# A fifth gate pair in the seven-product form, and GpSimd's share of the attention's elementwise work

## The chip, the cores and the metric

The kernel runs on one core of a Trainium2 chip. The metric is the device time of one execution in microseconds; less is better. The engines named below are PE (TensorE, the matmuls) with PEld (its weight loads), DVE (VectorE), ACT (ScalarE), POOL (GpSimd) and SP, whose queue issues nearly all DMAs.

## The reference

One decoder block on x of 1024 tokens by 1024 features, all float32:

```python
h = rms_norm(x, ln1_g)
proj = h @ w_in + b_in            # 1024 x 6400
rq, rk, rv, rg, aq, ak, av, gate_a, gate_b = jnp.split(proj, SPLIT_IDX, axis=-1)
ry = head_group_norm(retention_chunkwise(rotary(rq), rotary(rk), rv), ret_norm_g)
branch_a = (silu(rg) * ry) @ w_ret_out
ay = sliding_window_sink_attention(rotary(aq), rotary(ak), av, attn_sinks)
branch_b = ay @ w_attn_out
merged = sigmoid(gate_a) * branch_a + sigmoid(gate_b) * branch_b
x = x + merged @ w_out
h2 = rms_norm(x, ln2_g)
x = x + (silu(h2 @ w_ffn_gate) * (h2 @ w_ffn_up)) @ w_ffn_down
return rms_norm(x, lnf_g)
```

The attention has 16 query heads of 64 on 2 key/value heads, blocks of 128 queries against 256 keys (the block's own and the one before), a window of 128 and a learned sink for each head. The two gates have 1024 columns each, that is 16 groups of 128.

## The kernel before

**Products.** A float32 operand is kept as a high half (rounded to the matmul's fp32r) and a low half (the difference). A product is three matmuls: high by high, high by low, low by high. Weights are split after their load: `split` (L129) lets ACT write the high half (L130) and DVE the low (L133). `dense_g` (L176) does this for one group of 128 columns: load (L146), split, then for each half of the tokens 24 matmuls of 512 columns (`mm_g`, L157 to L159) and an evacuation. It is a generator: each `yield`, every three matmuls, is a step that other work can be put between.

**Stages.** By the trace: norm and the attention's k and v to 44 us; q of the first quad of heads to about 88; the attention to about 333, and what is left of its filling to 359; the retention's v from 359 to 435, and then, to 624, pairs of 128 columns (retention q and k, the swish gate, and some of the gates), both in a form with seven products of halves of the operands where eight would be usual (L841 for the pairs, their columns in `cols`, L599); the retention itself, the output projections and the FFN. Ten pairs run in the second of the seven-product stages: eight for the retention, two for gates 2 to 5.

**The attention.** 32 units, 4 quads of heads by 8 blocks; unit (g,b) is block b of quad g, and its tiles bear these digits (pv13 belongs to unit (1,3), sc16 to (1,6)). A unit goes through

- `u_scores`: four score products (PE L459, L460), the copy of the sink into each row (POOL L451), the masked row reduction (DVE L463), four exponentials with row sums (ACT L466), the reciprocal (DVE L469), and four scalings: columns 0 and 2 on DVE (L474), 1 and 3 on ACT (L472);
- `u_transpose`: eight transposes on PE (L484), the split by ACT (L487) and DVE (L488);
- `u_values`: the value products (PE L497, L498), copies and sums by ACT (L501, L502) and DVE (L503, L504), and a split back into q's place (L506, L507).

The loop runs unit i−1's transposes, unit i's scores, some steps of filling, and unit i−1's values. The **filling** (`Fill`, L187) is a list of generators: the q of the next quad (`quad_q`, L384: its weights L395 to L402, then 96 matmuls, the bias L409, the rotation on DVE L419 to L424, a split L425 to L428, a store L430 and a reload L432 through memory) and the gates (`gate`, L509: 48 matmuls, tanh L513, a store L514). Before a new quad begins, `until` runs the filling up to that quad's q. The weights of the filling are emitted under a raised priority (`AHEAD`); the order of each engine's instructions follows from these priorities, and each engine runs its own in order, as SP does its DMAs.

Two buffers (`wr`) hold raw weights, three PSUM banks (`acc`) the filling's results.

Of the kernel before, what the change touches and what calls it, by code (L numbers as in the profile page):

```python
# [14 lines left out]
ALU = mybir.AluOpType  # L15

P = 128
D = 1024
S = 1024
NB = S // P  # L20
# [10 lines left out]
C_RQ, C_RK, C_RV, C_RG, C_AQ, C_AK, C_AV, C_GA, C_GB = (  # L31
    0, 512, 1024, 2048, 3072, 4096, 4224, 4352, 5376)


def f32(t):
    return t.bitcast(F32)
# [3 lines left out]
def hybrid_block(ctx: ExitStack, tc: tile.TileContext, x, ln1_g, w_in, b_in, ret_norm_g, w_ret_out,  # L40
                 attn_sinks, w_attn_out, w_out, ln2_g, w_gate, w_up, w_down, lnf_g,
                 c_ident, c_atab, c_rtab, c_amask, c_rmask, c_rcol, out):
    nc = tc.nc
    x = x[0]
    out = out[0]
    w_in, w_ret_out, w_attn_out, w_out = w_in[0], w_ret_out[0], w_attn_out[0], w_out[0]
# [79 lines left out]

    held = []

    def split(raw, hi, lo, hold=False):  # L129
        nc.scalar.copy(hi, raw)  # L130

        def low():
            return nc.vector.tensor_tensor(out=lo, in0=raw, in1=f32(hi), op=ALU.subtract)  # L133
        if hold:
            held.append(low)
        else:
            return low()
# [2 lines left out]
        while held:  # L140
            held.pop(0)()

    def slab(src, col, name):
        with tc.high_priority(offset=AHEAD):
            raw = raw_slab([8, P], name)
            nc.sync.dma_start(raw, src[:, col:col + P].rearrange("(k p) n -> p k n", p=P))  # L146
            hi, lo = hl_tiles([8, P], name)
            split(raw, hi, lo)
        return hi, lo

    def mm_g(pt, w, X, c0, n=512):
# [21 lines left out]
        for i, (wt, k, u) in enumerate(todo):  # L173
            nc.tensor.matmul(pt, wt[:, k, :], X[k // 4][:, 2 * (k % 4) + u, c0:c0 + n], start=(i == 0), stop=(i == 23))

    def dense_g(src, col, X, evac, name):  # L176
        w = slab(src, col, name)
        for half in range(2):
            pt = acc(f"acc_{name}_{half}")
            yield from mm_g(pt, w, X, half * 512)  # L180
            evac(half, pt)
            yield
# [64 lines left out]
    for t in range(NB):  # L247
        if t > 1:
            nc.sync.dma_start(xs[:, t, :], x[t * P:(t + 1) * P, :])
        if 1 <= t <= 2:  # L250
            raw = raw_slab([8, P], f"kv{t}")
# [3 lines left out]
    H = [big(A, "A", 0, "h0"), big(A, "A", 1, "h1")]  # L255
# [45 lines left out]
    with tc.tile_pool(name="gt", bufs=1, side="right") as gt, tc.tile_pool(name="w1", bufs=1) as w1:  # L301
# [83 lines left out]
        def quad_q(g):  # L385
            if g % 2 == 0:
                big(B, "B", g // 2, f"q{g}")
            Bt = B[g // 2]
            jb = (g % 2) * 4
            w = [hl_tiles([8, P], f"aq{g}{z}") for z in range(2)]  # L390
            hp = tc.high_priority(offset=AHEAD)
            hp.__enter__()
            for kk in range(2):
                raw = raw_slab([4, 256], f"aq{g}{kk}")
                nc.sync.dma_start(raw, w_in[kk * 512:kk * 512 + 512, C_AQ + g * 256:C_AQ + g * 256 + 256]  # L395
                                  .rearrange("(k p) n -> p k n", p=P))
                rv_ = raw.rearrange("p k (j z e) -> p k z j e", j=4, z=2, e=32)
                for z in range(2):
                    hi = w[z][0][:, kk * 4:kk * 4 + 4, :].rearrange("p k (j e) -> p k j e", e=32)
                    lo = w[z][1][:, kk * 4:kk * 4 + 4, :].rearrange("p k (j e) -> p k j e", e=32)  # L400
                    nc.scalar.copy(hi, rv_[:, :, z])
                    nc.vector.tensor_tensor(out=lo, in0=rv_[:, :, z], in1=f32(hi), op=ALU.subtract)  # L402
            hp.__exit__(None, None, None)
            ab = {}
            for z, half in ((0, 0), (0, 1), (1, 0), (1, 1)):
                pt = acc(f"aq{g}{z}{half}")
                yield from mm_g(pt, w[z], H, half * 512)
                t = r512("ra" if z == 0 else "rb", 2 - z, f"q{g}{z}{half}")
                nc.scalar.activation(t, pt, AF.Identity, bias=bcol[:, QB + 4 * z + g:QB + 4 * z + g + 1], scale=1.0)  # L409
                ab[z, half] = t  # L410
                if z == 0:
                    yield
                    continue
                c = slice(half * 512, half * 512 + 512)
                a, b = ab[0, half], t
                stg = w1.tile([P, 4, 512], F32, tag="stg", bufs=1, name=f"stg{g}{half}")
                s0, s1, s2, s3 = (stg[:, i, :] for i in range(4))
                cos, sin = atab[:, 0, c], atab[:, 1, c]
                nc.vector.tensor_tensor(out=s2, in0=a, in1=cos, op=ALU.mult)  # L419
                nc.vector.tensor_tensor(out=s1, in0=b, in1=sin, op=ALU.mult)  # L420
                nc.vector.tensor_tensor(out=s2, in0=s2, in1=s1, op=ALU.subtract)
                nc.vector.tensor_tensor(out=s0, in0=a, in1=sin, op=ALU.mult)
                nc.vector.tensor_tensor(out=s3, in0=b, in1=cos, op=ALU.mult)
                nc.vector.tensor_tensor(out=s3, in0=s3, in1=s0, op=ALU.add)  # L424
                nc.scalar.activation(s0.bitcast(F32R), s2, AF.Copy)  # L425
                nc.vector.tensor_tensor(out=s2.bitcast(F32R), in0=s2, in1=s0, op=ALU.subtract)
                nc.scalar.activation(s1.bitcast(F32R), s3, AF.Copy)
                nc.vector.tensor_tensor(out=s3.bitcast(F32R), in0=s3, in1=s1, op=ALU.subtract)  # L428
                qd = q_d[2 * g + half]
                nc.sync.dma_start(qd, stg)  # L430
                for r in range(4):
                    nc.sync.dma_start(f32(Bt[r * 32:r * 32 + 32, jb:jb + 4, c]),  # L432
                                      qd[:, r, :].rearrange("(j e) c -> e j c", e=32))
                yield
# [9 lines left out]
        def u_scores(u):  # L444
# [23 lines left out]
            rd = tiny.tile([P, 4], F32, tag="rd", name=f"rd{g}{b}")  # L468
            nc.vector.reciprocal(rd, den)  # L469
            for j in range(4):  # L470
                if j % 2:
                    nc.scalar.activation(sc[:, j, 0:nk], sc[:, j, 0:nk], AF.Copy, scale=rd[:, j:j + 1])  # L472
                else:
                    nc.vector.tensor_scalar(out=sc[:, j, 0:nk], in0=sc[:, j, 0:nk], scalar1=rd[:, j:j + 1],  # L474
                                            scalar2=None, op0=ALU.mult)

        def u_transpose(u):
            g, b, nk, Bt, jb, qc = geo(u)
# [30 lines left out]
        def gate(n):  # L509

            def evac(half, pt):
                t = gt.tile([P, 512], F32, tag="st", bufs=2, name=f"tb{n}{half}")
                nc.scalar.activation(t, pt, AF.Tanh, bias=bhalf[:, n:n + 1], scale=0.5)  # L513
                nc.sync.dma_start(tb_d[n, :, half * 512:half * 512 + 512], t)  # L514
            return dense_g(w_in, C_GA + n * P, H, evac, f"g{n}")

        run(quad_q(0))
        order = list(range(6, 16))
        gens = []
        for g in range(4):  # L520
            gens += [quad_q(g + 1)] if g < 3 else []
            gens += [gate(n) for n in (order[2 * g:2 * g + 2] if g < 3 else order[6:] + [0, 1])]
        fl = Fill(gens)
        NU = 4 * NB
        fl.step(20)
        left = 32 * 8 - 8 - 20
        for i in range(NU + 1):
            if i % NB == 0 and 0 < i < NU:
                fl.until(3 * (i // NB - 1) + 1)
            if i > 0:  # L530
                u_transpose(i - 1)
            if i < NU:
# [63 lines left out]
        return [kq.tile([P] + shape, F32, tag=t, name=f"{name}{t}") for t in ("kT", "qT")]  # L596

    cols = [c for h in range(RH) for c in ((C_RK, C_RQ, C_RK + 256, C_RQ + 256)[h], C_RG + 256 * h)]
    cols += [C_GA + 256, C_GA + 512]  # L599
    NW = len(cols)  # L600

    with tc.tile_pool(name="rvp", bufs=1) as rvp:
# [706 lines left out]
    X = {}  # L1309
# [384 lines left out]
```

## Time and profile before

| | us |
|---|---|
| three runs | 1582.56, 1584.97, 1584.98 |
| median | 1584.97 |
| span of the profiled execution | 1583.3 |

No other time than its span is given for the profiled execution. In the windows, a row gives a stretch in us from the span's start, its length, and the busy time of each engine with its number of instructions. A busy time counts overlaps of neighbouring instructions once. A row of the groups gives line, engine, operation, tiles (out<-in), shapes, count, then total us and mean ns of one, then the idle time ahead of them and what ended it. A row of the waits gives who waited, for whom, the total, how often, and the longest.

### The profile page before, as it was taken

What the parts mean: (1) busy time and instruction counts of PE and PEld (TensorE: products, weight loads), DVE (VectorE), ACT (ScalarE), POOL (GpSimd) and SP (SyncE); (2) the same over time, 40 slices, a digit from 0 to 9 for tenths busy, and PEclk for the clock granted to TensorE, in tenths of its full rate; (3) what the DMA queues carried; (4) which work ended last, traced back from release to release, by engine and by line L of the source; (5) the groups of instructions that cost most, each with busy time, mean ns of one, the idle gap of its engine ahead of it and who ended that gap; (6) DMA issues with size and microseconds to landing.
All of it is one profiled execution on the core that took longest, in us unless ns stands there. A gap on an engine that the chain in (4) does not pass through costs nothing.

```text
span 1583.3 us, 20873 instructions
## 1 busy us (share of the span) xinstructions
PE 1570.7 (99%) x7483; PEld 1307.1 (83%) x7483; DVE 990.2 (63%) x1776; ACT 720.7 (46%) x1446; POOL 354.9 (22%) x303
## 2 busy tenths in 40 slices
PE   9999999999999999999999999999999999999998
PEld 8887888888888888888888888888888888888886
DVE  6469978777657663878544369444444444678656
ACT  5258877844233333544221256333333333344445
POOL 2000000000055441000000013555555555100001
PEclk9999999999999999999999999999999999999999
DMA  6564655440364455654545102333333333762333
GB/s 204 157 176 124 205 193 150 143 140 34 126 225 150 134 166 184 229 189 156 177 149 199 54 0 74 106 104 106 112 105 100 101 110 109 285 250 84 98 103 124
DMA packets 148886, 223.13 MB, mean 141 GB/s; under 512 B 9195, under 2 KB 81709, under 8 KB 147246
## 3 DMA queue, kind: packets, MB, share of 16 engines
q1 hardware_dynamic: 148780, 221.79, 43.3%
q8 instruction: 59, 0.97, 0.3%
q14 instruction: 45, 0.37, 0.1%
q10 hardware_dynamic: 2, 0.00, 0.0%
HBM read 149.67 MB, written 67.37 MB: 137 GB/s over the span
## 4 chain that ended last, share of the span: by engine, by line
PE 90%; ACT 6%; DVE 3%; issue 1%; POOL 0%; POOLq 0%; ACTq 0%; DVEq 0%
PE fA L1337 15%; PE fB L1337 8%; PE dA L1618 7%; PE wA L841 7%; PE dxP L1618 6%; PE fC L1337 4%; PE wB L841 3%; PE va L686 3%; ACT sc L466 2%; PE acc_g L157 2%; PE vP L686 2%; PE acc_g L158 2%; PE acc_g L159 2%; PE wo L1277 2%; PE wo L1276 2%; PE acc_ba L159 2%
## 5 line engine op out<-in xcount | busy, mean ns | idle before, releaser
L1618 PE MATMUL dA<-dwP,daP 128*128 128x512 f32 x528 | 120.6, 389 | 0.0
L1618 PEld LDWEIGHTS dA<-dwP,daP 128*128 128x128 f32 x528 | 99.0, 188 | 20.7 <-DVE dwP L133 0.2
L1618 PE MATMUL dxP<-dwP,daP 128*128 128x512 f32 x396 | 90.2, 389 | 0.0
L1618 PEld LDWEIGHTS dxP<-dwP,daP 128*128 128x128 f32 x396 | 74.3, 188 | 15.4
L157 PE MATMUL acc_g<-h,wh_g 128*128 128x512 f32 x192 | 75.5, 393 | 0.1
L158 PE MATMUL acc_g<-h,wh_g 128*128 128x512 f32 x192 | 75.2, 392 | 0.0
L159 PE MATMUL acc_g<-h,wl_g 128*128 128x512 f32 x192 | 75.1, 393 | 0.0
L466 ACT ACTIVATE sc<-sc,nm 128x257 f32<-128x257 f32 (+1 forms) x128 | 62.5, 492 | 27.1 <-DVE nm L463 26.7
L451 POOL COPY sc<-nsink 128x4 f32<-128x4 f32 x32 | 13.1, 412 | 274.4 <-PE pT L484 157.1
L1406 POOL TENSOR_TENSOR xf<-xf 128x512 f32<-128x512 f32 x40 | 61.2, 1531 | 30.4 <-issue 28.9
L1348 POOL TENSOR_TENSOR xf<-xf 128x512 f32<-128x512 f32 x33 | 49.4, 1496 | 54.3 <-ACT t_1P L130 22.4
L463 DVE CUSTOM_DVE_ANT_0 sc<-s,amask,nsink 128x256 f32<-128x256 f32 (+1 forms) x128 | 54.1, 461 | 9.8 <-PE s L460 9.5
L1358 ACT COPY xf<-fA 128x512 f32<-128x512 f32 x44 | 25.7, 586 | 74.4 <-PE fA L1337 74.4
L133 DVE TENSOR_TENSOR dwP<-wd,dwP 128x512 fp32r<-128x512 f32 x77 | 52.8, 685 | 6.0 <-ACT dwP L130 6.0
L130 ACT CAST dwP<-wd 128x512 fp32r<-128x512 f32 x77 | 47.4, 616 | 9.4 <-PE dA L1618 7.1
L157 PE MATMUL acc_bb<-ay,wh_bb 128*128 128x512 f32 x128 | 51.2, 400 | 0.0
L1523 POOL TENSOR_TENSOR rs_f<-tot,mhalf 128x1 f32<-128x1 f32 x8 | 4.8, 606 | 205.4 <-DVE tot L1520 205.4
L158 PE MATMUL acc_bb<-ay,wh_bb 128*128 128x512 f32 x128 | 50.3, 393 | 0.0
L159 PE MATMUL aq<-h,wl_aq 128*128 128x512 f32 x128 | 50.2, 392 | 0.0
L157 PE MATMUL aq<-h,wh_aq 128*128 128x512 f32 x128 | 50.1, 392 | 0.0
L158 PE MATMUL aq<-h,wh_aq 128*128 128x512 f32 x128 | 50.1, 391 | 0.0
L159 PE MATMUL acc_bb<-ay,wl_bb 128*128 128x512 f32 x128 | 50.1, 391 | 0.0
(794 smaller groups left out, 4356.9 us busy)
## 6 DMA issues: line engine op xcount, KB each, us to landing
act_d<-xf SPq DMA_DIRECT2D x77, 256.0 KB, 2.1
daP<-act_d SPq DMA_DIRECT2D x21, 512.0 KB
q_d<-stg SPq DMA_DIRECT2D x8, 1024.0 KB
q<-q_d SPq DMA_DIRECT2D x32, 256.0 KB, 6.5
ay_d<-q SPq DMA_DIRECT2D x8, 1024.0 KB
ay<-ay_d SPq DMA_DIRECT2D x4, 2048.0 KB, 14.2
wr_daP<-act_d SPq DMA_DIRECT2D x14, 512.0 KB, 3.7
wr_g<-in_w_in SPq DMA_DIRECT2D x12, 512.0 KB, 5.9
```

What stands on the lines that cost most here:

```text
L133: return nc.vector.tensor_tensor(out=lo, in0=raw, in1=f32(hi), op=ALU.subtract)
L157: nc.tensor.matmul(pt, hi[:, k, :], xh, start=(k == 0), stop=False)
L158: nc.tensor.matmul(pt, hi[:, k, :], xl, start=False, stop=False)
L159: nc.tensor.matmul(pt, lo[:, k, :], xh, start=False, stop=(k == 7))
L463: nc.vector.tensor_tensor_reduce(out=sc[:, j, 0:nk], in0=pt[:, jj * 256:jj * 256 + nk], in1=mk, scale=1.0, scalar=nsink[:, 4 * g + j:4 * g ...
L466: nc.scalar.activation(sc[:, j, 0:nk + 1], sc[:, j, 0:nk + 1], AF.Exp, scale=-1.0, bias=nm[:, j:j + 1], accum_out=den[:, j:j + 1])
L686: nc.tensor.matmul(vbanks[pr][tt], x_[:, c], w[:, u, :], start=(fresh and k + z == 0), stop=(k == 3 and z == 2), skip_group_check=not fresh)
L841: nc.tensor.matmul(pt, o[:, w, k, :], v, start=(first and k + z == 0), stop=(k == 3 and z == 2), skip_group_check=not first)
L1337: nc.tensor.matmul(pt, o[:, w, k, :], v, start=(first and k + z == 0), stop=(k == 3 and z == 2), skip_group_check=not first)
L1348: nc.gpsimd.tensor_tensor(out=dst[q], in0=dst[q], in1=sg[q], op=ALU.mult)
L1406: nc.gpsimd.tensor_tensor(out=o, in0=a, in1=b, op=op)
L1618: nc.tensor.matmul(banks[tt], a[:, u, c], w[:, v, :], start=(fresh and f + z == 0), stop=(f == NP - 1 and z == 2), skip_group_check=not fresh)
```

## The change

- Gates 0 and 1 leave the filling and become an eleventh pair in the seven-product stage, behind gates 2 to 5.
- The filling's list is laid out anew: q of quad 1, gate 6, q of quad 2, gates 7 and 8, q of quad 3, gate 9, then gates 10 to 15. Before it was q of quad 1, gates 6 and 7, q of quad 2, gates 8 and 9, q of quad 3, and the rest. The number of steps spread over the units falls from 228 to 196, and `until` gets fitting numbers.
- The low halves of the gates' weights and of the q of quads 1 to 3 go from DVE to GpSimd.
- Of the rotation of quads 1 to 3, the second output (two products and a sum) goes to GpSimd; the first stays on DVE.
- Of a unit's four scalings GpSimd takes column 3, ACT keeps column 1, DVE 0 and 2.

From L426 on, a line of before stands one line lower after.

```diff
-    def split(raw, hi, lo, hold=False):
+    def split(raw, hi, lo, hold=False, eng=None):
         nc.scalar.copy(hi, raw)
 
         def low():
-            return nc.vector.tensor_tensor(out=lo, in0=raw, in1=f32(hi), op=ALU.subtract)
+            return (eng or nc.vector).tensor_tensor(out=lo, in0=raw, in1=f32(hi), op=ALU.subtract)
...
                     nc.scalar.copy(hi, rv_[:, :, z])
-                    nc.vector.tensor_tensor(out=lo, in0=rv_[:, :, z], in1=f32(hi), op=ALU.subtract)
+                    (nc.gpsimd if g else nc.vector).tensor_tensor(out=lo, in0=rv_[:, :, z], in1=f32(hi), op=ALU.subtract)
...
+                second = nc.gpsimd if g else nc.vector
+                second.tensor_tensor(out=s3, in0=b, in1=cos, op=ALU.mult)
+                nc.vector.tensor_tensor(out=s1, in0=b, in1=sin, op=ALU.mult)
                 nc.vector.tensor_tensor(out=s2, in0=a, in1=cos, op=ALU.mult)
-                nc.vector.tensor_tensor(out=s1, in0=b, in1=sin, op=ALU.mult)
+                second.tensor_tensor(out=s0, in0=a, in1=sin, op=ALU.mult)
                 nc.vector.tensor_tensor(out=s2, in0=s2, in1=s1, op=ALU.subtract)
-                nc.vector.tensor_tensor(out=s0, in0=a, in1=sin, op=ALU.mult)
-                nc.vector.tensor_tensor(out=s3, in0=b, in1=cos, op=ALU.mult)
-                nc.vector.tensor_tensor(out=s3, in0=s3, in1=s0, op=ALU.add)
+                second.tensor_tensor(out=s3, in0=s3, in1=s0, op=ALU.add)
...
             for j in range(4):
-                if j % 2:
+                if j == 1:
                     nc.scalar.activation(sc[:, j, 0:nk], sc[:, j, 0:nk], AF.Copy, scale=rd[:, j:j + 1])
                 else:
-                    nc.vector.tensor_scalar(out=sc[:, j, 0:nk], in0=sc[:, j, 0:nk], scalar1=rd[:, j:j + 1],
-                                            scalar2=None, op0=ALU.mult)
+                    (nc.gpsimd if j == 3 else nc.vector).tensor_scalar(out=sc[:, j, 0:nk], in0=sc[:, j, 0:nk],
+                                                                       scalar1=rd[:, j:j + 1], scalar2=None, op0=ALU.mult)
...
-            return dense_g(w_in, C_GA + n * P, H, evac, f"g{n}")
+            return dense_g(w_in, C_GA + n * P, H, evac, f"g{n}", nc.gpsimd)
...
-        for g in range(4):
-            gens += [quad_q(g + 1)] if g < 3 else []
-            gens += [gate(n) for n in (order[2 * g:2 * g + 2] if g < 3 else order[6:] + [0, 1])]
+        for g in range(3):
+            gens += [quad_q(g + 1)] + [gate(n) for n in order[g + g // 2:g + 1 + (g + 1) // 2]]
+        gens += [gate(n) for n in order[4:]]
...
-        left = 32 * 8 - 8 - 20
+        left = 32 * 3 + 16 * len(order) - 40 - 20
         for i in range(NU + 1):
             if i % NB == 0 and 0 < i < NU:
-                fl.until(3 * (i // NB - 1) + 1)
+                fl.until((0, 1, 3, 6)[i // NB])
...
-    cols += [C_GA + 256, C_GA + 512]
+    cols += [C_GA + 256 * i for i in range(3)]
```

Between, `slab` and `dense_g` hand `eng` on to `split`.

The rows below are instructions in their engines' order: line, operation, out<-in by the program's names, shape. PE before, around the values of unit (1,3): `acc_g9` is gate 9's result, `wh_g9` and `wl_g9` its weights' halves, `pv13` the unit's values, `s150` scores of unit (1,5).

```order
L460 MATMUL s150_1996<-kst_180,q0_625 128x256
L157 MATMUL acc_g9_0_2038<-h0_109,wh_g9_2034 128x512
L158 MATMUL acc_g9_0_2038<-h0_109,wh_g9_2034 128x512
L498 MATMUL pv13_1961<-pl130_1896,vst_181 128x512
L497 MATMUL pv13_1961<-ph131_1904,vst_181 128x512
L159 MATMUL acc_g9_0_2038<-h0_109,wl_g9_2035 128x512
L498 MATMUL pv13_1961<-pl131_1905,vst_181 128x512
```

PE after, two units later, at the values of unit (1,5), with the first matmuls on gate 8's weights.

```order
L498 MATMUL pv15_2078<-ph150_2015,vst_181 128x512
L499 MATMUL pv15_2078<-pl150_2016,vst_181 128x512
L498 MATMUL pv15_2078<-ph151_2024,vst_181 128x512
L499 MATMUL pv15_2078<-pl151_2025,vst_181 128x512
L460 MATMUL s171_2121<-kst_180,q0_625 128x256
L157 MATMUL acc_g8_0_1917<-h0_109,wh_g8_1913 128x512
L158 MATMUL acc_g8_0_1917<-h0_109,wh_g8_1913 128x512
L157 MATMUL acc_g8_1_2062<-h0_109,wh_g8_1913 128x512
L158 MATMUL acc_g8_1_2062<-h0_109,wh_g8_1913 128x512
L461 MATMUL s171_2121<-kst_180,q0_625 128x256
L159 MATMUL acc_g8_0_1917<-h0_109,wl_g8_1914 128x512
```

Gate matmuls stood between the products of unit (1,3) before. After, between the last product of `pv12` and the first of `acc_g8_0`, PE has 3 matmuls of gate 7, then only the units (1,3) to (1,7)'s own rows: with those 3, 15 matmuls of 512 columns, 25 of 256 and 24 transposes.

ACT before, around the casts of gate 8's and gate 9's weights (`tm` copies and `q` belong to a unit's values, `ph` to its transposes, `sc` are exponentials):

```order
L466 ACTIVATE sc12_1728,den12_1731<-sc12_1728,nm12_1730 128x257
L487 CAST ph110_1715<-pT110_1710 128x512
L487 CAST ph111_1724<-pT111_1719 128x512
L130 CAST wh_g8_1855<-wr_g8_1853 128x1024
L425 ACTIVATE stg20_1680<-stg20_1680 128x512
L427 ACTIVATE stg20_1680<-stg20_1680 128x512
L506 CAST q0_625<-tm10_1703 128x2x128
L466 ACTIVATE sc12_1728,den12_1731<-sc12_1728,nm12_1730 128x257
L409 ACTIVATE q211_1777<-aq211_1696,bcol_86 128x512
L130 CAST wh_g9_2034<-wr_g9_2032 128x1024
```

ACT after, at gate 8's cast:

```order
L473 ACTIVATE sc15_1952<-sc15_1952,rd15_1974 128x256
L502 COPY tm14_2003<-pv14_1998 64x256
L503 COPY tm14_2003<-pv14_1998 64x256
L467 ACTIVATE sc16_2028,den16_2031<-sc16_2028,nm16_2030 128x257
L488 CAST ph150_2015<-pT150_2010 128x512
L488 CAST ph151_2024<-pT151_2019 128x512
L507 CAST q0_625<-tm14_2003 128x2x128
L467 ACTIVATE sc16_2028,den16_2031<-sc16_2028,nm16_2030 128x257
L130 CAST wh_g8_1913<-wr_g8_1911 128x1024
```

Gate 8's cast stood behind the `ph` casts of unit (1,1) before; after, it stands behind those of unit (1,5).

POOL had only the sink copies in the attention. After, around gate 8's low half, its rows are these (`sc` with L475 is a unit's fourth scaling, `stg21` the rotation of quad 2's second half):

```order
L475 TENSOR_SCALAR sc12_1684<-sc12_1684,rd12_1706 128x256
L420 TENSOR_TENSOR stg21_1717<-q211_1715,atab_176 128x512
L423 TENSOR_TENSOR stg21_1717<-q201_1481,atab_176 128x512
L425 TENSOR_TENSOR stg21_1717<-stg21_1717 128x512
L452 COPY sc14_1865<-nsink_85 128x4
L475 TENSOR_SCALAR sc13_1785<-sc13_1785,rd13_1807 128x256
L452 COPY sc15_1952<-nsink_85 128x4
L475 TENSOR_SCALAR sc14_1865<-sc14_1865,rd14_1887 128x256
L452 COPY sc16_2028<-nsink_85 128x4
L475 TENSOR_SCALAR sc15_1952<-sc15_1952,rd15_1974 128x256
L452 COPY sc17_2108<-nsink_85 128x4
L133 TENSOR_TENSOR wl_g8_1914<-wr_g8_1911,wh_g8_1913 128x1024
```

A unit's scaling and the sink copy of the unit two further on now share POOL's order with the rotation and the low halves.

More of the change, by code (lines that the diff above doesn't have):

```diff
@@ L141, in release, with slab @@
             held.pop(0)()
-    def slab(src, col, name):
+    def slab(src, col, name, eng=None):
         with tc.high_priority(offset=AHEAD):
@@ L147, in slab @@
             hi, lo = hl_tiles([8, P], name)
-            split(raw, hi, lo)
+            split(raw, hi, lo, eng=eng)
         return hi, lo
@@ L174, in mm_halves, with dense_g @@
             nc.tensor.matmul(pt, wt[:, k, :], X[k // 4][:, 2 * (k % 4) + u, c0:c0 + n], start=(i == 0), stop=(i == 23))
-    def dense_g(src, col, X, evac, name):
-        w = slab(src, col, name)
+    def dense_g(src, col, X, evac, name, eng=None):
+        w = slab(src, col, name, eng)
         for half in range(2):
```

## The prediction, made before the result was known

> **What bounds the kernel now.** I read the page's busy shares and the chain that ended last first, then the busy time of each engine by stage, then the waits inside the attention.
>
> ```profile
> span 1583.3 us, 20873 instructions
> PE 1570.7 (99%) x7483; PEld 1307.1 (83%) x7483; DVE 990.2 (63%) x1776; ACT 720.7 (46%) x1446; POOL 354.9 (22%) x303
> PE 90%; ACT 6%; DVE 3%; issue 1%; POOL 0%; POOLq 0%; ACTq 0%; DVEq 0%
> ```
>
> TensorE is busy 99% of the span and is 90% of the chain. A change can therefore do two things: alter the number of matmuls, or make TensorE wait. The profiled execution has a span of 1583.3 us; the median of the runs is 1584.97, 1.7 above it. I add the change to the span and carry these 1.7 along.
>
> Busy time by stage shows what lies beside TensorE. The columns are the window, its length, then PE, PEld, DVE, ACT and POOL, with the granted clock behind them.
>
> ```profile
> 102.97:209.83 106.86, 105.73 (x563) 85.79 (x563) 97.35 (x290) 93.36 (x265) 6.84 (x16) 1.00 0.55 163
> 209.83:324.68 114.85, 112.91 (x601) 94.58 (x600) 89.76 (x265) 89.83 (x246) 5.96 (x14) 1.00 0.48 159
> 552.54:571.58 19.04, 19.04 (x86) 15.77 (x85) 12.17 (x13) 7.31 (x13) 8.71 (x6) 1.00 0.42 120
> ```
>
> The first two rows are the attention's two halves, cut at the first transposes of units (0,0), (2,0) and (3,7). There DVE and ACT are busy for 91% and 87%, then 78%, of the time: close behind TensorE. The third row is one pair in the seven-product form: TensorE never stops, nothing else is near it. The clock is 1.00 in all of them, so it does not enter.
>
> ```profile
> PEld pT L484 <- ACT sc L472: 2.8, 12, 0.4
> PE pT L484 <- ACT sc L472: 1.2, 3, 0.7
> ```
>
> These rows of the waits over the attention (total us, times, longest) show that the transposes wait for ACT's scalings, but never for more than 0.7 us at a time. The filling matmuls of the gates and of the next q cover the units' chains; that cover is what the change makes smaller.
>
> **Matmuls: −2.72 us.**
>
> ```profile
> 358.91 10.91 PE va L686 x48
> 38.84 2.88 PE ak L174 x24
> 158.06 1.10 PE L484 MATMUL pT<-ident,sc 128*128 128x128 f32 x8
> 158.92 0.48 PE L157 MATMUL aq<-h,wh_aq 128*128 128x512 f32 x1
> ```
>
> The chain's first row gives 10.91/48 = 0.227 us a matmul of 512 columns, the second 0.12 for 256, and the two timeline rows (158.92 − 158.06)/8 = 0.108 for a transpose. Gates 0 and 1 leave the filling: 2 × 48 matmuls, −96 × 0.227 = −21.76. The eleventh pair adds one whole period of 19.04, the window above. TensorE is full there and the other engines are at most 64% busy, so I take the whole period, 19.04. Net −2.72. If a period stretched because its one more store and load came late, it would cost tenths; TensorE's full window speaks against more.
>
> **Where the cover goes: gate 8, +7.1 us.** TensorE runs its rows in order, and the order after has one place without filling. Between the last matmul of unit (1,2)'s values and gate 8's first matmul stand 3 matmuls of gate 7 and three whole units: 15 matmuls of 512, 25 of 256 and 24 transposes. That is 15 × 0.227 + 25 × 0.12 + 24 × 0.108 = 9.0 us of rows. ACT must in this time get from unit (1,2)'s copies to gate 8's cast, and its order after has between them 3 pairs of copies, 12 exponentials, 3 scalings, 3 casts of q, 6 of ph, one tanh and the cast.
>
> ```profile
> 152.34 0.37 ACT L501 COPY tm<-pv 64x256 f32<-64x256 f32 x1
> 152.72 0.36 ACT L502 COPY tm<-pv 64x256 f32<-64x256 f32 x1
> 153.11 0.70 ACT L472 ACTIVATE sc<-sc,rd 128x128 f32<-128x128 f32 x2
> 153.71 0.50 ACT L466 ACTIVATE sc<-sc,nm 128x257 f32<-128x257 f32 x1
> 154.11 0.19 ACT L466 ACTIVATION_READ_ACCUMULATOR sc<-sc,nm 128x1 f32 x1
> 154.21 0.50 ACT L466 ACTIVATE sc<-sc,nm 128x257 f32<-128x257 f32 x1
> 154.61 0.19 ACT L466 ACTIVATION_READ_ACCUMULATOR sc<-sc,nm 128x1 f32 x1
> 154.70 0.39 ACT L506 CAST q<-tm 128x256 fp32r<-128x256 f32 x1
> 155.00 0.58 ACT L487 CAST ph<-pT 128x512 fp32r<-128x512 f32 x1
> 155.47 0.51 ACT L466 ACTIVATE sc<-sc,nm 128x257 f32<-128x257 f32 x1
> ...
> 157.44 0.91 ACT L472 ACTIVATE sc<-sc,rd 128x256 f32<-128x256 f32 x2
> ...
> 160.21 1.06 ACT L130 CAST wh_g<-wr_g 128x1024 fp32r<-128x1024 f32 x1
> 161.16 0.64 ACT L425 ACTIVATE stg<-stg 128x512 fp32r<-128x512 f32 x1
> ```
>
> Neighbouring ACT rows overlap, so I take start to start: copies 0.38 and 0.39, an exponential with its read-out 0.50, a cast of q 0.30, of ph 0.47, gate 8's cast 0.95; a scaling about 0.41 (half of the 0.91 less the overlap). For the tanh I take 0.58, its mean below less the usual 0.1. The sum is 3 × 0.77 + 12 × 0.50 + 3 × 0.41 + 3 × 0.30 + 6 × 0.47 + 0.58 + 0.95 = 14.8 us. So even if ACT never waits itself, gate 8's first matmul comes 14.8 − 9.0 = 5.8 us late.
>
> ```profile
> L513 ACT ACTIVATE tb<-acc_g,bhalf 128x512 f32<-128x512 f32 x15 | 10.1, 675 | 3.7 <-PE acc_g L159 3.7
> L555 POOL TENSOR_TENSOR t<-wrx_f,wr_f 128x512 f32<-128x512 f32 x20 | 25.8, 1290 | 2.9 <-DMA wrx_f<-in_w_ffn_gate 1.5
> L133 DVE TENSOR_TENSOR wl_g<-wr_g,wh_g 128x1024 fp32r<-128x1024 f32 x12 | 14.6, 1220 | 7.0 <-ACT wh_g L130 6.9
> L402 DVE TENSOR_TENSOR wl_aq<-wr_aq,wh_aq 128x512 fp32r<-128x512 f32 x16 | 10.6, 686 | 11.3 <-ACT wh_aq L401 11.3
> wr_g<-in_w_in SPq DMA_DIRECT2D x12, 512.0 KB, 5.9
> ```
>
> Then the low half, now on GpSimd. No row of before has a 128x1024 of GpSimd; the 128x512 takes 1.29, and on DVE the larger takes 1.220/0.686 as long as the smaller, so 2.29 by estimate. Its bounds are DVE's 1.22 and two of the longer GpSimd rows, 3.5. Gate 8's first low matmul stands 4 matmuls of 512 and one of 256 behind the first high one, 1.02 us. So 2.29 − 1.02 = 1.27 more: 5.8 + 1.3 = **7.1**, with 6.0 and 8.3 by these bounds, and about 10 if the units, left without cover, go at the pace of their own chains. In before, gate 8's and gate 9's casts stand behind unit (1,1), two units earlier, and this wait isn't there. SP issues gate 8's load after one store of q more than before, but some 30 rows of ACT lie between that store's last input and the cast, about 14 us, and a load lands in 5.9: hidden.
>
> **Quad 3's start: +1.4 us.** The same sum for quad 3's first weights, from unit (1,6)'s values: ACT has 0.77 of copies, 0.41, 0.58, two ph casts 0.94, 0.30, an exponential 0.39 and the cast 0.52, together 3.9; TensorE has 16 × 0.108 + 4 × 0.227 + 5 × 0.12 = 3.2 of rows. That is 0.7 late, and the low half of 1.29 against 0.57 of rows in between adds 0.7. Below, 0, if gate 8's wait has let ACT run ahead; above, 3. All other weights stand 4 us or more ahead of their use in the order after.
>
> **What is relieved: 0.** DVE loses 10 low halves of 1.22, 12 of 0.686, 18 rotation steps of that size, ACT 32 scalings; GpSimd gets all these. The new GpSimd scaling (128x256) has no row; it lies between the sink copy below, 0.43, and a 128x512, 1.29.
>
> ```profile
> L451 POOL COPY sc<-nsink 128x4 f32<-128x4 f32 x30 | 12.8, 427 | 271.9 <-PE pT L484 157.1 <-ACT tm L502 26.3 <-ACT ph L487 23.5
> ```
>
>  What this could save is the present overhead: TensorE's rows from (0,0) to (2,0) count 322 × 0.227 + 104 × 0.12 + 136 × 0.108 = 100.3 of 106.86, and 109.8 of 114.85 after it, so 6.6 and 5.0 are lost now. Filling falls by 51 and 42 matmuls there, so the chains have less cover for what ACT and DVE were relieved of. From −6.8 to +5; I take 0, since the two pull against each other in every unit.
>
> The sum is −2.72 + 7.1 + 1.4 = +5.8: 1589.1 for the span, **1590.8** beside the median. Its own range is 1588 to 1594.
>
> **The rivals.** (1) *The relief decides, 1584.0 or less.* DVE and ACT are the engines whose rows stand close to TensorE's in the first half; with fewer of them the loss of 6.6 and 5.0 shrinks. If it goes by 6.8, the sum is −1.0; from 5.8 on the kernel is not slower, and all of the 11.6 would give 1579. For it speak the waits on the scalings quoted above; against it, that these two rows sum to only 4.0.
>
> (2) *GpSimd is late, about 1596.*
>
> ```profile
> 449.12 1.30 POOL L555 TENSOR_TENSOR wp<-wp,wt 128x512 f32<-128x512 f32 x1
> 449.18 1.79 DVE L133 TENSOR_TENSOR w1P<-wr_wp,w1P 128x512 fp32r<-128x512 f32 x1 [1.85 <-ACT w1P L130]
> 450.38 1.74 POOL L812 TENSOR_TENSOR xw<-xw,rtabqT 128x512 f32<-128x512 f32 x1
> 450.89 1.78 DVE L813 TENSOR_TENSOR r<-r,rtabkT 128x512 f32<-128x512 f32 x1
> 452.60 0.68 DVE L133 TENSOR_TENSOR w0P<-wr_wp,w0P 128x512 fp32r<-128x512 f32 x1
> ```
>
> ```profile
> L463 DVE CUSTOM_DVE_ANT_0 sc<-s,amask,nsink 128x256 f32<-128x256 f32 x111 | 48.8, 478 | 1.0 <-PE s L460 0.7
> L469 DVE RECIPROCAL rd<-den 128x4 f32<-128x4 f32 x31 | 5.5, 176 | 11.2 <-ACT sc L466 10.8
> ```
>
> A DVE step on two SBUF operands takes 0.68 alone and 1.78 beside GpSimd: 1.1 more each. The attention has nearly no GpSimd work today and gets 40 steps of this kind. A scaling behind one of them in GpSimd's order can be late: unit to unit the order leaves 5.1 us from a unit's last score to its transposes, and reduction, four exponentials and reciprocal take about 2.7, the scaling up to 1.29, leaving 1.1; a low half of 2.29 ahead of it makes it 1.2 late. Four such places of some 22 give +5 on top of the forecast. Against it: most low halves wait for a cast that comes at a free time.
>
> [...]
>
> (3) *Only the matmul count shows, 1582.3.* Gate 8's cast could run earlier than my sum if TensorE is behind anyway at that place and ACT has time to catch up. Then −2.72 is all.
>
> **How the numbers follow.** A measurement of this kernel tells about 0.2%, 3.2 us, from no change. I give the forecast 0.50, rival 1 0.25, rival 2 0.15, rival 3 0.10. Slower by over 0.2% (above 1588.1) are the forecast but for 0.04, rival 2, and 0.03 of rival 1: 0.64. Faster (below 1581.8) are 0.10 of rival 1 and 0.02 of rival 3. The rest, 0.24, is within. The range runs from 1581.5, which takes in rival 3 and the smaller half of rival 1, to 1597, rival 2; about 0.1 is left out below and 0.08 above.
>
> **What would show it.** In the profile after: one wait of TensorE of 5 to 10 us between 155 and 175 us, at the first matmul on gate 8's weights, released by ACT's cast and then by GpSimd's low half; a smaller one at quad 3's; the pair's period at 19.04, eleven times. Rival 1 shows as the halves' excess over the matmuls' sum falling without such a gap; rival 2 as transposes released by GpSimd's scaling and DVE's two-operand steps at 1.3 to 1.8 us. The forecast is wrong if the longest wait of TensorE in the attention stays under 2 us.

## The result, and the profile after

The changed kernel takes 1609.7 us (median; 1607.62 to 1610.54) beside 1584.23 before: 1.0162 times as long, with a 95% interval of 1.0148 to 1.0177. It is slower by 25.5 us, where +5.8 had been forecast and the range ended at 1597.

The page after, with the busy shares and the chain that ended last:

```profile
span 1605.8 us, 20923 instructions
PE 1574.9 (98%) x7471; PEld 1305.0 (81%) x7471; DVE 989.1 (62%) x1744; ACT 711.8 (44%) x1422; POOL 456.3 (28%) x379
PE 91%; DVE 4%; ACT 3%; issue 1%; POOL 1%; DMA 1%; SPq 0%; POOLq 0%; ACTq 0%; DVEq 0%
```

POOL is busy for 101 us more. DVE, from which most of that work was taken, is busy for 1 us less: over the whole span it got no relief.

Windows of the same three stretches after: the attention's first half, its second, and one pair of the seven-product stage (window, length, then PE, PEld, DVE, ACT, POOL):

```profile
101.45:213.00 111.55, 95.88 (x497) 73.40 (x497) 95.25 (x269) 83.24 (x239) 44.36 (x49) 1.00 0.46 135
213.00:330.00 117.00, 112.28 (x577) 91.24 (x577) 91.27 (x251) 84.31 (x235) 44.39 (x44) 0.99 0.48 156
559.60:578.70 19.10, 19.10 (x86) 15.79 (x85) 12.76 (x16) 5.56 (x10) 8.69 (x6) 1.00 0.46 126
```

The windows of the attention are cut a little otherwise than before, by the places where the units now stand, so they show shares. The granted clock, which stands behind the engines, is 1.00 and 0.99. TensorE was busy for 99% of the first half and is now for 86%. The pair's period is as forecast, 19.1 and no gap in it.

Where the attention ends shows the balance. The chain's row of the first matmuls of the next stage:

```profile
363.14 10.96 PE va L687 x48
```

It stood at 358.91. So the attention, with 21.8 us of matmuls fewer, ends 4.2 later, and what came before its first transposes is 1.5 shorter in this execution. Some 27 us were given back inside it. The eleventh pair's 19 come on top.

**What DVE's steps take.** Groups of DVE in the attention, first before, then after (columns: total us and mean ns of one behind the first bar):

```profile
L474 DVE TENSOR_SCALAR sc<-sc,rd 128x256 f32<-128x256 f32 x56 | 17.3, 349 | 0.5
L422 DVE TENSOR_TENSOR stg<-q,atab 128x512 f32<-128x512 f32 x6 | 4.1, 685 | 0.0
L488 DVE TENSOR_TENSOR pl<-pT,ph 128x512 fp32r<-128x512 f32 x60 | 40.5, 687 | 1.8 <-ACT ph L487 1.0
```

```profile
L475 DVE TENSOR_SCALAR sc<-sc,rd 128x256 f32<-128x256 f32 x56 | 27.2, 526 | 0.5
L422 DVE TENSOR_TENSOR stg<-q,atab 128x512 f32<-128x512 f32 x6 | 7.4, 1226 | 0.6 <-ACT q L409 0.6
L421 DVE TENSOR_TENSOR stg<-q,atab 128x512 f32<-128x512 f32 x6 | 6.7, 1110 | 0.0
L489 DVE TENSOR_TENSOR pl<-pT,ph 128x512 fp32r<-128x512 f32 x60 | 40.2, 686 | 8.7 <-ACT ph L488 8.0
```

The scalings went from 349 to 526 ns, the rotation's products from 0.685 to 1.1 and 1.2 us. The step that reads its first operand from PSUM (`pl<-pT,ph`) kept 0.686. With the other stretched groups of that window (the sum of the rotation, the residues of q and of the rotation, and `wv`), DVE's steps are 24 us longer in all. What was taken from it is 10 × 1.219 + 12 × 0.684 + 18 × 0.684 = 32.7 us. Three quarters of the relief went into longer steps.

GpSimd's own groups after:

```profile
L475 POOL TENSOR_SCALAR sc<-sc,rd 128x256 f32<-128x256 f32 x28 | 28.6, 1023 | 77.1 <-DVE rd L470 72.7 <-PE acc_g L159 4.4
L133 POOL TENSOR_TENSOR wl_g<-wr_g,wh_g 128x1024 fp32r<-128x1024 f32 x9 | 22.4, 2489 | 24.7 <-ACT wh_g L130 24.7
```

A scaling takes 1.02 us there, three times what it took on DVE, and a gate's low half 2.49 (estimated 2.29).

**How it reaches TensorE.** The timeline after, rotation of quad 1's second half, without the weight loads and other rows between:

```profile
120.59 1.29 POOL L420 TENSOR_TENSOR stg<-q,atab 128x512 f32<-128x512 f32 x1
121.33 1.10 DVE L421 TENSOR_TENSOR stg<-q,atab 128x512 f32<-128x512 f32 x1
121.85 1.74 POOL L423 TENSOR_TENSOR stg<-q,atab 128x512 f32<-128x512 f32 x1
122.36 1.77 DVE L422 TENSOR_TENSOR stg<-q,atab 128x512 f32<-128x512 f32 x1
123.66 1.60 POOL L425 TENSOR_TENSOR stg<-stg 128x512 f32<-128x512 f32 x1
124.05 1.50 DVE L508 TENSOR_TENSOR q<-tm,q 128x256 fp32r<-128x256 f32 x1
...
125.47 0.68 DVE L424 TENSOR_TENSOR stg<-stg 128x512 f32<-128x512 f32 x1
126.07 0.68 DVE L489 TENSOR_TENSOR pl<-pT,ph 128x512 fp32r<-128x512 f32 x1
126.23 0.63 ACT L426 ACTIVATE stg<-stg 128x512 fp32r<-128x512 f32 x1 [4.04 <-POOL stg L425]
...
126.81 0.50 PE L499 MATMUL pv<-pl,vst 128*128 128x512 f32 x1 [2.07 <-DVE pl L489]
```

Each of the three DVE rows on two SBUF operands that start beside a GpSimd row ends 0.3 to 0.6 us behind that row's end: DVE's two products take 1.10 and 1.77 us beside GpSimd's 1.29 and 1.74, where DVE took 0.68 in before. Behind them in DVE's order stands `pl`, which the unit's values wait for, and TensorE loses 2.07 us. ACT waits as well: its cast of the rotated q (L426) stands ahead of exponentials in its order. The view names GpSimd's sum (L425) for the 4.04 us, but that ended at 125.26, and DVE's own sum (L424) at 126.15, 0.08 before the cast. ACT waits five times ahead of this cast, 11.6 us in all, where before it never did; in four of the five DVE's sum ends last. In the waits of TensorE over the attention (total us, times, longest) these rows are among the largest:

```profile
PEld pv L499 <- DVE pl L489: 9.3, 15, 2.5
...
PE pv L498 <- DVE tm L505: 5.5, 4, 2.6
...
PE pv L499 <- DVE pl L489: 4.4, 8, 2.1
...
PE pT L485 <- DVE sc L475: 3.4, 5, 1.3
...
PEld aq L159 <- POOL wl_aq L402: 2.4, 2, 1.6
...
PEld pT L485 <- POOL sc L475: 1.7, 10, 0.2
```

TensorE's waits for DVE are far longer than those for GpSimd's own results.

**Gate 8.** The last matmul of unit (1,2)'s values, and the first and the first low matmul of gate 8:

```profile
174.69 0.43 PE L499 MATMUL pv<-pl,vst 128*128 128x512 f32 x1
...
191.17 0.40 PE L157 MATMUL acc_g<-h,wh_g 128*128 128x512 f32 x1
...
193.19 0.50 PE L159 MATMUL acc_g<-h,wl_g 128*128 128x512 f32 x1 [0.81 <-POOL wl_g L133]
```

16.5 us lie between the first two, for 9.0 of rows; to the low matmul it is 18.5 for 10.0. So 8.5 are lost where 7.1 had been forecast, though not in one wait: gate 8's first matmul itself waits for nothing, the rows of the units ahead of it have eight marked waits of 0.2 to 0.95 us, and the low matmul waits 0.81. The window from the last filling matmul ahead of the stretch to gate 8's first (columns as above) shows what bounds it:

```profile
175.42:191.17 15.75, 12.08 (x63) 7.97 (x62) 15.26 (x49) 15.33 (x47) 3.93 (x7) 1.00 0.96 271
```

DVE and ACT are both busy for 97% of it. Without filling, the units go at the pace of these two. What the stretch costs the whole kernel is asked below.

### The profile page after: what moved, and what is told of

It is laid out like the page before. It is cut to its first block, busy times and chain, and to the rows that moved or that the text cites. A ratio compares the mean times of both kernels' runs of the same rounds, so it can differ in the third digit from the quotient of the medians.

```text
span 1605.8 us, 20923 instructions
## 1 busy us (share of the span) xinstructions
PE 1574.9 (98%) x7471; PEld 1305.0 (81%) x7471; DVE 989.1 (62%) x1744; ACT 711.8 (44%) x1422; POOL 456.3 (28%) x379
## 4 chain that ended last, share of the span: by engine, by line
PE 91%; DVE 4%; ACT 3%; issue 1%; POOL 1%; DMA 1%; SPq 0%; POOLq 0%; ACTq 0%; DVEq 0%
PE fA L1338 15%; PE fB L1338 7%; PE wA L842 7%; PE dA L1619 7%; PE dxP L1619 6%; PE fC L1338 4%; PE wB L842 4%; PE va L687 3%; PE vP L687 2%; PE wC L842 2%; PE wo L1277 2%; PE wo L1276 2%; PE acc_ba L158 2%; PE acc_ba L157 2%; PE wo L1278 2%; PE acc_g L159 2%
## 5 line engine op out<-in xcount | busy, mean ns | idle before, releaser
L467 ACT ACTIVATE sc<-sc,nm 128x257 f32<-128x257 f32 (+1 forms) x128 | 62.6, 492 | 23.6 <-DVE nm L464 23.4
L159 PE MATMUL acc_g<-h,wl_g 128*128 128x512 f32 x160 | 63.0, 395 | 0.8 <-POOL wl_g L133 0.8
L158 PE MATMUL acc_g<-h,wh_g 128*128 128x512 f32 x160 | 63.2, 395 | 0.0
L157 PE MATMUL acc_g<-h,wh_g 128*128 128x512 f32 x160 | 63.1, 394 | 0.0
L475 POOL TENSOR_SCALAR sc<-sc,rd 128x256 f32<-128x256 f32 (+1 forms) x32 | 32.1, 1004 | 88.4 <-DVE rd L470 84.0
L556 POOL TENSOR_TENSOR wr_f<-wr_f 128x512 f32<-128x512 f32 x20 | 30.3, 1513 | 79.0 <-DVE t_4P L133 8.7
L1007 POOL TENSOR_TENSOR grs<-gve,mhalf 128x2 f32<-128x2 f32 x16 | 11.3, 704 | 145.1 <-DVE gve L1005 145.1
L556 POOL TENSOR_TENSOR wr_wp<-wr_wp 128x512 f32<-128x512 f32 x11 | 17.9, 1624 | 119.6 <-issue 92.6
L157 PE MATMUL acc_bb<-ay,wh_bb 128*128 128x512 f32 x128 | 50.9, 399 | 0.0
```

What stands on the lines that cost most here:

```text
L157: nc.tensor.matmul(pt, hi[:, k, :], xh, start=(k == 0), stop=False)
L158: nc.tensor.matmul(pt, hi[:, k, :], xl, start=False, stop=False)
L159: nc.tensor.matmul(pt, lo[:, k, :], xh, start=False, stop=(k == 7))
L467: nc.scalar.activation(sc[:, j, 0:nk + 1], sc[:, j, 0:nk + 1], AF.Exp, scale=-1.0, bias=nm[:, j:j + 1], accum_out=den[:, j:j + 1])
```

## The experiments

Three theories stood against each other: L, that GpSimd's work stops DVE and TensorE waits for DVE; C, that 96 filling matmuls fewer leave the units without cover; G, that gate 8's late weights are most of it. Ratios have their 95% interval; "before" was run beside each.

**pair_alone**: the eleventh pair and the new list, with all of GpSimd's new work undone.

```diff
-            return dense_g(w_in, C_GA + n * P, H, evac, f"g{n}", nc.gpsimd)
+            return dense_g(w_in, C_GA + n * P, H, evac, f"g{n}")
...
-                    (nc.gpsimd if g else nc.vector).tensor_tensor(out=lo, ...
+                    nc.vector.tensor_tensor(out=lo, ...
-                second = nc.gpsimd if g else nc.vector
+                second = nc.vector
-                if j == 1:
+                if j % 2:
```

> The fifth pair and the new list of the filling as in the change; all of GpSimd's new work (low halves, half of the rotation, one scaling in four) goes back to DVE and ACT. Gate 8's cast stands ahead of unit (1,2) again, so its gap is gone. Theory L (GpSimd's work stops DVE, and TensorE waits for DVE): 1582 to 1587. Theory C (96 filling matmuls fewer leave the units without cover): 1597 to 1606. Theory G (gate 8's gap is most of the loss): 1598 to 1602 cannot be, since the gap is gone too; G gives about 1584.

Measured: 1590.63, ratio 1.0040 (1.0025 to 1.0055), +6.2 us. Neither L's 1582 to 1587 nor C's 1597 to 1606. GpSimd's part is the larger one, but the thinner filling is not free: 6.2 + 2.7 of saved matmuls are 8.9 given back. The gap at gate 8 isn't there, but in its place is another: from 166.46 to 173.72 no filling matmul starts, and the rows in it are worth 2.0 us.

**pool_alone**: the change's GpSimd work with the filling, list and ten pairs of before.

```diff
-        for g in range(3):
-            gens += [quad_q(g + 1)] + [gate(n) for n in order[g + g // 2:g + 1 + (g + 1) // 2]]
-        gens += [gate(n) for n in order[4:]]
+        for g in range(4):
+            gens += [quad_q(g + 1)] if g < 3 else []
+            gens += [gate(n) for n in (order[2 * g:2 * g + 2] if g < 3 else order[6:] + [0, 1])]
...
-    cols += [C_GA + 256 * i for i in range(3)]
+    cols += [C_GA + 256, C_GA + 512]
```

> GpSimd's new work as in the change, with the filling of 12 gates, the list and the ten pairs of before. Gate 8's cast stands two units earlier again. Theory L: 1596 to 1604 (the 24 us by which DVE's steps were longer in the changed kernel's attention, less what more cover hides). Theory C: 1582 to 1587. Theory G: 1582 to 1587.

Measured: 1601.63, ratio 1.0112 (1.0097 to 1.0127), +17.2 us, as L has it. No matmul has been taken away and gate 8 isn't late, so C and G give nothing here. The two parts add to 23.4 of the 25.5.

Part of the 17.2 is TensorE's clock. Two of TensorE's waits in this run, then a window (columns as above) behind the second of them, and a matmul in it:

```profile
129.47 0.79 PE L499 MATMUL pv<-pl,vst 128*128 128x512 f32 x1 [3.34 <-DVE pl L489]
...
185.43 2.03 PE L485 MATMUL pT<-ident,sc 128*128 128x128 f32 x8 [1.25 <-DVE sc L475]
```

```profile
186.00:190.00 4.00, 4.00 (x14) 3.30 (x14) 3.45 (x11) 2.98 (x8) 0.26 (x2) 0.50 0.01 2
```

```profile
188.11 0.63 PE L158 MATMUL acc_g<-h,wh_g 128*128 128x512 f32 x1
```

The granted clock is 0.50 there, and the matmuls of 512 columns follow each other after 0.43 us in place of 0.23. There are three such stretches in this run's attention. What they cost can be estimated from windows of 1 us between 90 and 385: the clock's shortfall times TensorE's busy time is 5.9 us here, 2.7 in pair_alone, 1.7 in the change, and nothing in before. These are estimates from single profiled executions, and the figures differ, so that the two parts add up so nearly is in part chance.

**no_rot, no_low, no_scale**: one piece of GpSimd's work undone at a time, by the lines shown for pair_alone (`second`; the two low halves; `j % 2`).

> The change with the whole rotation back on DVE; low halves and one scaling in four stay on GpSimd. In the order gate 8's cast then stands ahead of unit (1,2)'s values, without a gap. Theory G: 1601 less the rest, that is the change less 8.5, 1601. Theory L: less 8.5 and less about 9 of the 24 us of DVE's longer steps, 1591 to 1596. Theory C: 1601.

> The change with the gates' and q's low halves on DVE again; half of the rotation and one scaling in four stay on GpSimd, and gate 8's gap stays in the order. Theory L: DVE takes 20 us of steps back but is stopped less; 1601 to 1606. Theory C and G: 1608 to 1611.

> The change with scalings 1 and 3 on ACT again; low halves and half of the rotation stay on GpSimd. Gate 8's gap stays in the order. Theory L: DVE's own scalings (0.53 in the change, 0.35 before) lose about half of their 12 us, 1602 to 1606. Theory C and G: no change against the changed kernel, 1608 to 1611.

Measured: 1600.96, 1602.83 and 1606.35; ratios 1.0106 (1.0089 to 1.0123), 1.0124 (1.0109 to 1.0139), 1.0141 (1.0126 to 1.0157). no_low lies inside L's range and no_scale 0.35 above its end; both lie below the 1608 to 1611 of G and C. no_rot lies 5 above L's, at the 1601 that G and C had for it, so it alone tells nothing apart (in its profile the slower clock costs 4.5 us by the estimate above). By the ratios' difference to the change's 1.0162, times 1584, undoing the rotation brings 8.9 us, the low halves 6.0, the scalings 3.3: 18.2 together, and undoing all of them (pair_alone) 19.3. No single piece is the culprit. How the 19 divide among them is less sure. no_rot has no stretch of over 5 us without filling, so its 8.9 hold what gate 8's stretch costs as well; in no_low that stretch is shorter (11.7 us for 7.0 of rows); and the interval of no_scale overlaps the change's. A likely reason why the rotation costs much for its 27 us on GpSimd (18 steps of about 1.5) is that its other half runs on DVE at the same moment, and why the scalings cost little for their 32 us, that they also take 32 steps off ACT; neither was tried apart.

**gap_closed**: the change, with gate 8's load and split at a higher priority.

```diff
     def slab(src, col, name, eng=None):
-        with tc.high_priority(offset=AHEAD):
+        with tc.high_priority(offset=300 if name == 'g8' else AHEAD):
```

> The change with gate 8's load and split emitted under a raised priority of 300 in place of 100, all else the same. In the order gate 8's cast then stands ahead of unit (1,1)'s copies and its first matmul two rows behind unit (1,2)'s values: the gap of 9 us of rows without filling is closed, and GpSimd's work is as in the change. If the late cast costs what it seems to in the changed kernel's trace (8.5): 1600 to 1603. If thin filling and a stopped DVE cost about the same there without it: 1606 to 1610.

Measured: 1606.95, ratio 1.0154 (1.0140 to 1.0167). The intervals of this and of the change overlap: by the ratios 1.3 us came back, by the medians 2.8. But the run does not do what was expected of its edit. Gate 8's matmuls are in their place, and the stretch without filling stands further on, ahead of quad 3's first weights:

```profile
202.88:217.40 14.52, 10.24 (x61) 7.65 (x59) 12.99 (x51) 13.43 (x45) 2.85 (x5) 1.00 0.27 100
```

Its rows are worth 8.0 us, so 6.5 are lost there in place of the 7 to 8.5 at gate 8. And where the filling now stands, TensorE still waits for DVE; its waits in 160 to 200 us:

```profile
PEld pv L499 <- DVE pl L489: 3.7, 2, 3.0
...
PE pv L499 <- DVE pl L489: 2.8, 2, 2.6
```

So gap_closed moves the gap and does not close it, and cannot tell what a gap costs. That such a gap isn't most of the loss is shown by pool_alone, which loses 17.2 us without one at gate 8.

**dum_set, dum_read, dum_read3**: the kernel before, plus GpSimd steps that nobody needs, during quad 0's units. A tiny step ties each group to its unit (`rds` keeps the unit's reciprocal), and `wk` is dead by then.

```diff
+            rds[u] = rd
...
+        nc.gpsimd.memset(wk[:, 6:8, :], 0.0)
...
+            if 0 < i <= NB:
+                nc.gpsimd.tensor_scalar(out=wk[:, 6, 0:1], in0=wk[:, 7, 0:1], scalar1=rds[i - 1][:, 0:1], scalar2=None, op0=ALU.mult)
+                for _ in range(6):                    # 3 in dum_read3
+                    nc.gpsimd.tensor_tensor(out=wk[:, 6, 0:512], in0=wk[:, 7, 0:512], in1=wk[:, 7, 512:1024], op=ALU.subtract)
+                    # dum_set instead: nc.gpsimd.memset(wk[:, 6, :], 0.0)
```

> The kernel before, with 48 subtractions of 128x512 on GpSimd during quad 0's units (six a unit, each group released by the unit's reciprocal) that read and write a buffer nobody else uses then; nobody waits for them but GpSimd's own sink copies. Every engine but GpSimd has the same order as in dum_set. Port (GpSimd holds what DVE's steps between SBUF operands need): DVE's scalings, rotation and low halves in that stretch are longer by 0.3 to 1.1 us each, those with a PSUM operand not; 4 to 12 above before. Queue (only steps that wait for GpSimd are late): no more than dum_set.

> As dum_read with memsets of 128x1024 in place of the subtractions: GpSimd is as busy, and writes, but reads nothing. Port, if reading matters: DVE's steps on two SBUF operands keep 0.68; within 2 of before. Port, if any GpSimd step holds it: as dum_read. Queue: as dum_read.

> As dum_read with three subtractions a unit in place of six, 24 in all: GpSimd then is busy for some 34 us there and its sink copies stand behind three steps at most. Port: DVE's steps between SBUF operands are still longer where the two meet, and ACT no longer waits for sink copies; 5 to 10 above before, half of what dum_read lost without those waits. Queue alone: within 2 of before.

Measured: dum_set 1588.4, ratio 1.0030 (1.0019 to 1.0041); dum_read 1609.35, 1.0164 (1.0149 to 1.0179); dum_read3 1597.27, 1.0083 (1.0066 to 1.0100). That is about +5, +26 and +14: more than expected each time. In dum_read part of it is another matter, since its sink copies came late behind six steps. The waits of ACT there:

```profile
ACT sc L467 <- POOL sc L452: 15.1, 5, 4.5
```

No such row stands among the waits of dum_set and dum_read3, so these two are compared. Groups of their stretch, dum_set first:

```profile
L538 POOL MEMSET wk<- 128x1024 f32 x48 | 46.1, 961 | 2.3
...
L476 DVE TENSOR_SCALAR sc<-sc,rd 128x256 f32<-128x256 f32 x28 | 14.0, 539 | 0.1
L509 DVE TENSOR_TENSOR q<-tm,q 128x256 fp32r<-128x256 f32 x14 | 5.8, 417 | 0.1
L422 DVE TENSOR_TENSOR stg<-q,atab 128x512 f32<-128x512 f32 x4 | 2.7, 683 | 0.0
```

```profile
L538 POOL TENSOR_TENSOR wk<-wk 128x512 f32<-128x512 f32 x24 | 35.8, 1493 | 1.9
...
L490 DVE TENSOR_TENSOR pl<-pT,ph 128x512 fp32r<-128x512 f32 x28 | 18.5, 685 | 0.5 <-ACT ph L489 0.2
L476 DVE TENSOR_SCALAR sc<-sc,rd 128x256 f32<-128x256 f32 x28 | 13.9, 536 | 0.1
L509 DVE TENSOR_TENSOR q<-tm,q 128x256 fp32r<-128x256 f32 x14 | 8.2, 584 | 0.1
L422 DVE TENSOR_TENSOR stg<-q,atab 128x512 f32<-128x512 f32 x3 | 3.2, 1052 | 0.0
```

GpSimd is busy longer with the memsets (46.1 against 35.8 us), and yet the subtractions cost 2.6 times as much. With the memsets, DVE's steps on two SBUF operands keep 0.683 and 0.417 in the mean (0.685 and 0.418 in before); with the subtractions these two groups take 1.05 and 0.58 (other groups of the kind take 0.68 to 1.05, as they meet a subtraction or not). The scaling, with one SBUF operand and a column, is stretched by both alike, from 0.349 to 0.54. The step with a PSUM operand (`pl<-pT,ph`) is stretched by neither, 0.684 and 0.685. So in these two runs the steps on two SBUF operands were longer beside the subtraction, which reads and writes SBUF, and not beside the memset, which only writes it, while the scaling was longer beside either; and no instruction of the kernel needs a result of these GpSimd steps. The transposes' waits for the scaling over these units, dum_set first:

```profile
PE pT L486 <- DVE sc L476: 3.1, 7, 0.8
```

```profile
PE pT L486 <- DVE sc L476: 6.3, 7, 2.8
```

What makes the steps longer no run shows: the Port of the expectations was a theory, and what the runs have for it is these durations.

**pair_tail, pair_208, pair_front**: the kernel before with the eleventh pair and without gates 0 and 1, in its own list; they differ in how the filling is spread.

```diff
-            gens += [gate(n) for n in (order[2 * g:2 * g + 2] if g < 3 else order[6:] + [0, 1])]
+            gens += [gate(n) for n in (order[2 * g:2 * g + 2] if g < 3 else order[6:])]
...
-        left = 32 * 8 - 8 - 20
+        left = 208      # pair_208; pair_tail keeps 228
...
+        # pair_front: the pace of 228 up to unit 17, then 208 in all
+        def pace(i):
+            return i * left // (NU + 1) if i <= 17 else 17 * left // (NU + 1) + (i - 17) * (208 - 17 * left // (NU + 1)) // (NU + 1 - 17)
-            fl.step((i + 1) * left // (NU + 1) - i * left // (NU + 1))
+            fl.step(pace(i + 1) - pace(i))
...
-    cols += [C_GA + 256, C_GA + 512]
+    cols += [C_GA + 256 * i for i in range(3)]
```

> The kernel before with the eleventh pair alone, and its filling laid out as before: the same list and pace, only gates 0 and 1 are missing at its end, so that 8 steps are left after the last unit instead of 40. If the loss of pair_alone came from thinner filling in the first half (theory C in small): 1581 to 1584, the -2.72 of the matmuls with nothing given back. If any 96 matmuls fewer cost their cover wherever they are taken: about 1590 as pair_alone.

> As pair_tail, with 208 steps spread over the units in place of 228, so that 28 steps are left after the last unit (before: 40, pair_tail: 8). pair_tail lost 12.3 in one wait after the attention, where the next stage's operands weren't ready; 20 more steps are 13.6 us of matmuls there. If that is all: 1582 to 1586. If the thinner filling costs as in pair_alone: 1587 to 1590.

> As pair_208, with the pace of before up to unit 17 and the 20 steps taken from the later units, where DVE and ACT are busy for 78% and not 91% of the time. 1581 to 1585: the matmuls' -2.72 with little given back; below before's median if the later units bear it. If any thinning costs: 1587.

Measured: pair_tail 1595.68, ratio 1.0072 (1.0055 to 1.0089), above both expectations. Its attention's halves have the length of before, but behind it stands one wait:

```profile
336.75 0.84 PE L686 MATMUL va<-vP,h 128*128 128x512 f32 x3
...
350.50 2.08 PE L686 MATMUL va<-vP,h 128*128 128x512 f32 x4 [12.01 <-DVE vP L133]
```

The 32 steps taken from the end had covered the next stage's preparation on DVE. The granted clock is 0.81 in the mean from 324 to 360 us, and the four matmuls behind the wait take 2.08 us, where three ahead of it took 0.84. pair_208, with 28 steps left there, has no such wait and takes 1586.68, 1.0015 (1.0006 to 1.0025; its ten runs spread from 1583 to 1587, so the medians lie further apart than the ratio says); pair_front 1582.44 beside 1583.07, ratio 0.9997 (0.9988 to 1.0006). So the same thinning costs something when the first half bears a share of it, much when all of it is taken from the end, and nothing measurable when the later units bear it. pair_front gives back about what the pair saves: no difference to before can be measured, and no version here is clearly faster.

## Why the prediction was wrong

- **Matmuls, −2.72: right.** The pair's period is 19.1 in the window after, and 96 matmuls have left the attention.
- **Gate 8, +7.1: about right where it was looked for.** 8.5 us are lost in that stretch, with ACT and DVE both full, as the sum of ACT's rows against TensorE's had it; but not in the one wait of 5 to 10 us that was to show it, and the longest wait of a matmul in the attention, 2.6 us, is for DVE's `tm`. What closing the gap alone would bring is not known, since gap_closed moved it.
- **Quad 3's start, +1.4: too small.** Its first low matmul waits 0.52 us for GpSimd's low half, where 0.7 had been put. In the stretch ahead of its first matmul (204.21 to 211.47, 4.4 of rows) some 2.8 more are lost; together that is a little over the 3 that the term had as its end.
- **"What is relieved: 0" is the step that failed.** It let the relief of DVE and ACT and the loss of cover cancel, with −6.8 to +5 as ends. It listed the steps that DVE loses, 32.7 us, as relief, and took the steps left to DVE at the durations of before. They did not keep them: 24 us came back as longer steps, and pool_alone shows +17.2 from GpSimd's part with no cover lost at all. With 17.2 in place of the 0 the sum would be +23.0, beside 25.5 measured. That it comes so near is in part luck: pair_alone shows that the thinner filling gives back 8.9 us, near the 8.5 of the gate 8 and quad 3 terms, also in an order that has its gap elsewhere.
- **Rival 2** had the right rows (1.78 beside 0.68), and then priced something else: four GpSimd scalings that come late, 5 us. TensorE waited little for GpSimd's results (1.6 us at the longest). The price was in DVE's steps. For these it had 1.1 us more each and 40 GpSimd steps on two SBUF operands, and nothing for them in its 1596; scalings, GpSimd's and DVE's, were left out of the 40, and of the 24 us found 11.8 are DVE's scalings (56 go from 0.349 to 0.526, 8 smaller ones from 0.28 to 0.52). The argument against it, that most low halves fall into free time, missed that DVE's steps are longer also where nobody waits for GpSimd's result: dum_read3 lost 14 us so.
- **The rate of exchange.** GpSimd's part costs 17 to 19 us for 24 of longer DVE steps, although 32.7 had been taken off DVE. DVE's busy time in the first half did not grow (97.35 us before, 95.25 after), so what costs is where the longer steps stand: ahead of `pl`, `tm` and the scalings that TensorE waits for. In before, DVE was busy for 91% of that half, which leaves such a step little room; that row stood in the prediction.
- **The clock, 1.00 and left out.** In the change this costs little, 1.7 us by the estimate above; in pool_alone it is a third of the loss.

Still open: how the 19 us of GpSimd's part divide between DVE's longer steps and GpSimd's own slower results (a scaling of 1.02 in place of 0.41). TensorE's waits put nearly all on DVE, and dum_read3 lost 14 where no result of GpSimd's added steps was needed, but no run gave GpSimd this work without DVE's longer steps. Whether the list or the pace makes pair_alone dearer than pair_208 was not tried apart.

## What to carry to other kernels

Moving elementwise work from a nearly full DVE to GpSimd moved less here than it seemed: of 32.7 us taken from DVE, 24 us came back as longer steps, a third of a us for each of the 72 GpSimd steps, and TensorE waited for those. Price such a move by the DVE steps that remain, and only then ask who waits for GpSimd. Filling that covers a dense stage has a rate and a place: of 32 steps, 20 taken from the later units and 12 from the end cost nothing measurable, and all 32 from the end made the kernel 12.6 us longer, where they had covered the next stage's preparation. And look whether an experiment that closes a gap has opened another.

## What the runs showed of the hardware

With GpSimd's memsets beside them (dum_set), DVE's steps on two SBUF operands kept their time (0.683 for 128x512); with its subtractions (dum_read3) groups of the same steps took up to 1.05 in the mean. A scaling by a column was stretched by both, from 0.349 to 0.54; a step with an operand in PSUM by neither (0.684 and 0.685). GpSimd's subtraction of 128x512 took 1.49 in dum_read3, where a group of that size in before took 1.29 (L555, `t<-wrx_f,wr_f`). The scaling of 128x256 takes 1.02 us on GpSimd beside DVE's 0.35. In pool_alone the granted clock was 0.50 from 186 to 190 us, behind a wait of TensorE of 1.25, and matmuls of 512 columns followed each other after 0.43 us in place of 0.23. In pair_tail it was 0.81 in the mean from 324 to 360 us, a stretch that holds the wait of 12.01. In the change it was 0.50 from 257 to 259 us, and 1.00 behind the wait of 2.07 at 126.81.
